# Where a kernel gathers the mean squares of its norms: launch, ends of layers and the second block moved in program order

## The chip, the cores and the metric

The kernel runs on one core of a Trainium2 chip. The metric is device time in microseconds (us) of one execution. Five engines work in order, each through its own row of instructions, and meet at semaphores: PE (TensorE, matmuls), DVE (VectorE), ACT (ScalarE), POOL (GpSimd) and SP (SyncE, which here issues the loads). A row of an engine that waits holds up everything behind it on that engine.

## What is computed

Two transformer blocks over 512 tokens of width 1024, in fp32. The first has two layers of feed-forward, mixed attention, feed-forward; the second has gated mixing, attention and a mixture of experts. Each part begins with a norm over a token's 1024 values:

```python
def rmsnorm(x, g):
    y = xf * lax.rsqrt(jnp.mean(xf * xf, axis=-1, keepdims=True) + EPS)
    return (y * g.astype(jnp.float32)).astype(x.dtype)

def swiglu(h, w_gate, w_up, w_down):
    return (jax.nn.silu(h @ w_gate) * (h @ w_up)) @ w_down

for l in range(DEPTH):          # first block, DEPTH = 2
    x = x + 0.5 * swiglu(rmsnorm(x, ffn1_norm[l]), ...)
    h = rmsnorm(x, mix_norm[l]); ...; x = x + o @ w_out[l]
    x = x + 0.5 * swiglu(rmsnorm(x, ffn2_norm[l]), ...)
return rmsnorm(x, final_norm)   # and the second block begins with rms_norm(h, attn_norm_g)
```

## The kernel before

The activations lie transposed: eight tiles `xT[k]` of 128 features by 512 tokens. The gain is multiplied into the tile before a product, and the factor per token (`rstd`, one over the root of the mean square) is multiplied into the product's result, so that matmuls may start before the norm is known.

An fp32 product is made of three matmuls. `split` turns an operand of 128x1024 into a rounded high part (ACT, `rounded<-base` or `rounded<-ws`, line 407) and the low part, the difference (DVE, line 408); the matmuls are high by high, high by low, low by high. "The cast" and "the low part" below are these two. Three pairs of buffers (`halves`) go round, so a cast waits until matmuls have read the pair three splits back.

**Feed-forward.** `ffn_duo` works on two blocks of columns of the gate and up weights, called a duo here, with seven products (24 matmuls 128x256 each) in place of eight: weights a11, a12, a21, a22 and their sums s1 = a21+a22, s2 = s1-a11, s3 = a11-a21, s4 = a12-s2 (DVE, line 604, `ws`). `cross_tile(q)` makes, for each pair of activation tiles, the operands B11, B2, T12, T34: scaled copies `yc` (ACT, 568), high parts (ACT, 579, 582, 587) and differences (DVE, 560). `down` then multiplies by the down weights (`pd`, lines 414 to 416, 128x512), makes the new tile (DVE, 707, 708), and calls `after(d)`: `norm_tile`, `cross_tile` or, at the end of the fourth feed-forward, `norm_tile2`.

**Norm.** `add_square` squares a tile on ACT (481) and adds it to a running sum on DVE (`acc`, 491). `mean_sq` sums over features with fp32 matmuls by a column of ones (`pstat`, 517), one for each 128 tokens. In the first feed-forward the eight squares are kept apart and all summed by PE: 32 matmuls, each of which shows as two records. `rsqrt` is eleven small operations on DVE (498 to 506). `spread` lays the factor over the partitions: `diag` on DVE (528), a matmul `pspread` on PE (533), a copy `rstd` on ACT (535).

**Launch.** `first_block` loads, in this order on SP's queue, two activation tiles and then half a weight block, four times over, then constants, then the second duo's weights. All eight cross tiles are issued first; then `ffn_duo` splits a11, a12 and s3 and starts three products (`begun`: p1, p2, p3, four steps k each). After three of the four steps comes the whole norm. Then follow s2, s1, s4 (product p4) and a22 (added to p3), and the second duo.

**Second block.** Its norm needs two sums of squares: that of x, and that of x times the final gain (`acc2`, squares at 1371). `second_block` projects k and v, then `gate_products` multiplies by four quarters of weights (`pgv`, 420 to 422: 24 matmuls 128x512 for each quarter), then come both `mean_sq`, two `rsqrt`, `spread`, and the next projections (`pin`, 414 to 416), whose results are multiplied by `rstd` (`ev`, DVE, 753).

Of the kernel before, what the change touches and what calls it, by code (L numbers as in the profile page):

```python
# [86 lines left out]
def layout_first(t):  # L87
    f = np.float32
    out = {}
    out["xt"] = np.ascontiguousarray(t["x"][0].T.reshape(8, 128, S))  # L90
# [221 lines left out]
class Build:  # L312
# [105 lines left out]
    def mm3m(self, out, xh, xl, wh, wl, first, last):  # L418
        mm = self.nc.tensor.matmul
        mm(out, xh, wh, start=first, stop=False)  # L420
        mm(out, xh, wl, start=False, stop=False)  # L421
        mm(out, xl, wh, start=False, stop=last)  # L422
# [54 lines left out]

    def add_square(self, k):

        sq = self.epage("sq") if self.acc_parts is None else self.buffer("sq0", 512, F32, "sq0", 8)  # L480
        self.nc.scalar.activation(sq, self.xT[k], AF.Square)
        if self.acc_parts is None:
            self.acc = self.add_sq(self.acc, sq)
        else:
            self.acc_parts.append(sq)
# [24 lines left out]
    def mean_sq(self, acc, n, eps=True):  # L510
# [3 lines left out]
        parts = acc if isinstance(acc, list) else [acc]  # L514
        for t in range(4):
            for i, a in enumerate(parts):
                nc.tensor.matmul(p[:, t:t + 1], a[:, 128 * t:128 * t + 128], self.ones[:, 0:1], start=i == 0,
                                 stop=i == len(parts) - 1)
# [18 lines left out]

    def rstd_of(self, acc, n):
        col = self.rsqrt(self.mean_sq(acc, n), 4)
# [6 lines left out]
    def start_norm(self):  # L546
        self.XH, self.XL, self.acc, self.acc_parts = [None] * 8, [None] * 8, None, None
# [9 lines left out]
    def cross_tile(self, q, g0):  # L557
# [11 lines left out]
        self.add_square(q)  # L569
# [24 lines left out]
    def ffn_duo(self, wa, wb, acc=None):  # L594
# [3 lines left out]
        a21, a11, a12, a22 = self.first_parts or [self.half_stage(w) for w in (wb[:, :1024], wa[:, :1024], wa[:, 1024:], wb[:, 1024:])]  # L598
        self.first_parts = None
        L, R = slice(0, 256), slice(256, 512)  # L600

        def add(x, y, op):
            z = self.buffer("ws", 1024, F32, "ws", N_WS)
            nc.vector.tensor_tensor(z, x, y, op=op)  # L604
            return z
# [22 lines left out]
        if acc is not None:  # L628
            s3 = add(a11, a21, ALU.subtract)
            begun = [(p1, parts(a11), self.B11, slice(0, 256)), (p2, parts(a12), self.B2, L),  # L630
                     (p3, parts(s3), self.T34, L)]
# [3 lines left out]
            with self.tc.issue_after(mm.ins):  # L635
                _, self.x_rstd = self.rstd_of(acc, D)
# [9 lines left out]
        if acc is None:  # L646
# [1543 lines left out]
```

## Time and profile before

| | |
|---|---|
| Time, median of 3 runs | 2774.12 us (2772.43 to 2777.51) |
| The profiled execution, its own time | 2776.47 us |
| Its span | 2774.6 us |
| Mean granted TensorE clock | 0.979 |
| PE, DVE, ACT busy | 95%, 76%, 51% of the span |

The span runs from the first to the last instruction that the profiler saw; the time holds a little more on both sides. A granted clock of 1.00 is 2.4 GHz, 0.50 is 1.2 GHz.

### The profile page before, as it was taken

Reading aid. Unit: us, or ns where it says so; the run is one execution under the profiler, and the core shown is the slowest. Engines: PE = TensorE matmul, PEld = TensorE weight load, DVE = VectorE, ACT = ScalarE, POOL = GpSimd, SP = SyncE. Lnnn points to the kernel's source line nnn. Section 1 sums busy time; section 2 is a strip of 40 time slices with the busy share of each in tenths; the row PEclk is TensorE's granted clock in tenths of the full one; section 3 lists DMA queues with packets and bytes.
Section 4 is the critical chain, followed back from the end, with each engine's and each line's share of the span. In section 5 each row is a group of like instructions: output and inputs, shape, how many; then the busy total and the mean of one; then the engine's idle time right before and its main releaser. Section 6 shows DMA issues by size and latency. Waiting matters only on the chain. (4 is left out here: it accounts for less than half of the span.)

```text
span 2774.6 us, 39572 instructions
## 1 busy us (share of the span) xinstructions
PE 2637.2 (95%) x15742; PEld 2267.3 (82%) x15742; DVE 2117.2 (76%) x2991; ACT 1401.6 (51%) x2137; POOL 261.8 (9%) x181
## 2 busy tenths in 40 slices
PE   6999999998999998999999999999998999789996
PEld 6999987766899897999987766999996888567774
DVE  6777775687877779787766787878785865579997
ACT  5434346455544355444446465534353644367874
POOL 0000001201000000000002110000000101134442
PEclk9999999999999999999999999999998999889998
DMA  3333331110342322333231111233232223679993
GB/s 126 123 102 88 120 114 63 61 54 22 101 159 92 107 92 84 113 101 107 73 116 55 56 54 33 92 111 94 97 99 96 88 77 120 229 281 365 375 369 124
DMA packets 83698, 335.35 MB, mean 121 GB/s; under 512 B 10414, under 2 KB 11878, under 8 KB 74552
## 3 DMA queue, kind: packets, MB, share of 16 engines
q1 hardware_dynamic: 77096, 315.15, 33.0%
q0 software_dynamic: 5264, 14.51, 1.5%
q8 instruction: 124, 2.03, 0.3%
q10 hardware_dynamic: 1152, 3.15, 0.3%
q14 instruction: 62, 0.51, 0.1%
HBM read 321.93 MB, written 17.84 MB: 122 GB/s over the span
## 5 line engine op out<-in xcount | busy, mean ns | idle before, releaser
L407 ACT CAST rounded<-base 128x1024 fp32r<-128x1024 f32 (+1 forms) x326 | 337.6, 1037 | 468.2 <-PE m L621 164.3
L621 PE MATMUL m<-xt,rounded 128*128 128x256 f32 x4224 | 537.8, 285 | 10.3 <-ACT u L651 5.1
L408 DVE TENSOR_TENSOR rounded<-base,rounded 128x1024 fp32r<-128x1024 f32 (+1 forms) x326 | 401.5, 1232 | 186.6 <-ACT rounded L407 185.5
L621 PEld LDWEIGHTS m<-xt,rounded 128*128 128x128 f32 x4224 | 519.7, 193 | 18.8 <-ACT u L651 6.6
L621 PE MATMUL m<-b,rounded 128*128 128x256 f32 x3168 | 412.6, 286 | 27.6 <-ACT rounded L407 21.8
L621 PEld LDWEIGHTS m<-b,rounded 128*128 128x128 f32 x3168 | 398.6, 194 | 33.7 <-ACT rounded L407 22.1
L408 DVE TENSOR_TENSOR rounded<-ws,rounded 128x1024 fp32r<-128x1024 f32 x176 | 215.3, 1223 | 99.7 <-ACT rounded L407 99.6
L407 ACT CAST rounded<-ws 128x1024 fp32r<-128x1024 f32 x176 | 184.9, 1050 | 197.1 <-PE m L621 108.3
L416 PE MATMUL pd<-h,rounded 128*128 128x512 f32 x704 | 274.8, 391 | 3.4 <-DVE rounded L408 3.4
L415 PE MATMUL pd<-h,rounded 128*128 128x512 f32 x704 | 275.4, 391 | 1.9 <-DVE h L796 1.7
L414 PE MATMUL pd<-h,rounded 128*128 128x512 f32 x704 | 274.6, 390 | 0.0
L414 PE MATMUL pin<-x,rounded 128*128 128x512 f32 x448 | 180.9, 404 | 0.7 <-ACT rstd L535 0.7
L416 PE MATMUL pin<-x,rounded 128*128 128x512 f32 x448 | 178.0, 397 | 0.0
L415 PE MATMUL pin<-x,rounded 128*128 128x512 f32 x448 | 177.4, 396 | 0.4 <-DVE x L476 0.4
L1958 DVE TENSOR_TENSOR rounded<-ew,rounded 128x1024 fp32r<-128x1024 f32 x105 | 167.5, 1614 | 8.2 <-ACT rounded L1956 6.5
L415 PEld LDWEIGHTS pd<-h,rounded 128*128 128x128 f32 x704 | 132.7, 188 | 30.2 <-DVE h L796 3.6
L416 PEld LDWEIGHTS pd<-h,rounded 128*128 128x128 f32 x704 | 132.7, 189 | 30.1 <-DVE rounded L408 3.8
L414 PEld LDWEIGHTS pd<-h,rounded 128*128 128x128 f32 x704 | 132.6, 188 | 26.6
L1956 ACT CAST rounded<-ew 128x1024 fp32r<-128x1024 f32 x119 | 124.9, 1053 | 39.7 <-PE peg L422 16.5
L604 DVE TENSOR_TENSOR ws<-base 128x1024 f32<-128x1024 f32 x88 | 105.8, 1220 | 15.0 <-DMA base<-w_gu 14.9
L1098 POOL TENSOR_TENSOR kpe<-kg,rope 32x512 f32<-32x512 f32 x2 | 2.9, 1459 | 1139.3 <-DVE kg L753 1139.3
L414 PEld LDWEIGHTS pin<-x,rounded 128*128 128x128 f32 x448 | 84.9, 190 | 20.9 <-issue 2.4
(492 smaller groups left out, 4867.4 us busy)
## 6 DMA issues: line engine op xcount, KB each, us to landing
base<-w_gu SPq DMA_DIRECT2D x176, 512.0 KB, 3.9
ew<-e_w SPq DMA_DIRECT2D x154, 512.0 KB, 7.4
base<-w_in SPq DMA_DIRECT2D x27, 1024.0 KB, 4.8
base<-w_dn SPq DMA_DIRECT2D x44, 512.0 KB, 3.7
base<-e_w SPq DMA_DIRECT2D x38, 512.0 KB, 8.5
base<-w_dn SPq DMA_DIRECT2D x16, 1024.0 KB, 4.8
base<-w_o SPq DMA_DIRECT2D x12, 1024.0 KB, 4.8
base<-w_dn SPq DMA_DIRECT2D x8, 768.0 KB, 4.1
```

The costliest lines, as they stand in the source:

```text
L407: nc.scalar.copy(hi[:, :cols], src)
L408: nc.vector.tensor_tensor(lo[:, :cols], src, hi[:, :cols], op=ALU.subtract)
L414: mm(out, wh, xh, start=first, stop=False)
L415: mm(out, wh, xl, start=False, stop=False)
L416: return mm(out, wl, xh, start=False, stop=last)
L604: nc.vector.tensor_tensor(z, x, y, op=op)
L621: mm = nc.tensor.matmul(o, w[:, q], x, start=first and j + k + m == 0, stop=k == 3 and m == 2, skip_group_check=True)
L1098: nc.gpsimd.tensor_tensor(out[r], t[r], self.cm[r], op=ALU.mult)
L1956: nc.scalar.copy(hi, src)
L1958: cut = eng.tensor_tensor(lo, src, hi, op=ALU.subtract)
```

## The change

In five parts. (1) At launch the squares of x come from token rows: a new input `xr` (x itself, four tiles of 128 tokens by 1024) is loaded behind the constants, and four ACT instructions square a row and sum it (`accum_out`). The eight squares of the tiles and the 32 `pstat` matmuls of the launch go. (2) The first three splits (a11, a12, s3) are issued between the cross tiles; the norm's chain and `pspread` stand after product p4. (3) The table of the function silu is loaded ahead of everything (`preload_act_table_set`). (4) At the end of a feed-forward all squares are made, and their sums issued after the last `down` (`add_squares`); after a mixer the sums are issued tile by tile, as before. (5) In the second block the sums of `acc2` are issued after the k and v projections, the `pstat` matmuls and the chain after the first half of `gate_products`, `pspread` after the second half.

```diff
+    def add_squares(self):
+        for sq in self.squares:
             self.acc = self.add_sq(self.acc, sq)
+        self.squares = []
...
+    def mean_sq_rows(self):
+        nc = self.nc
+        v, s = self.small([128, 4], "ms"), self.small([128, 4], "rs_a")
+        for t in range(4):
+            x = self.buffer("xr", 1024, F32, "xr", 2)
+            self.load(x, self.A["xr"][t])
+            with self.tc.issue_after(self.last_hi.ins):
+                nc.scalar.activation(x, x, AF.Square, accum_out=s[:, t:t + 1])
+        nc.vector.tensor_scalar(v, s, 1.0 / D, EPS, op0=ALU.mult, op1=ALU.add)
+        return v
...
-            with self.tc.issue_after(mm.ins):
-                _, self.x_rstd = self.rstd_of(acc, D)
+            if not self.begun:
+                with self.tc.issue_after(mm.ins):
+                    _, self.x_rstd = self.rstd_of(self.acc, D)
...
-        product(p4, parts(s4, u2_copy), self.B2, R)
+        mm = product(p4, parts(s4, u2_copy), self.B2, R)
+        if self.begun:
+            with self.tc.issue_after(mm.ins):
+                _, self.x_rstd = self.rstd_of(self.acc, D)
...
             while pieces:
                 down()
+            if last:
+                self.add_squares()
...
         self.load_constants()
+        self.nc.scalar.preload_act_table_set("silu_and_others")
...
         for q in range(8):
-            self.cross_tile(q, G_FFN1)
+            self.cross_tile(q, G_FFN1, False)
+            if q in (1, 3):
+                begun.append(self.split((a11, a12)[q // 2], 1024))
+            elif q == 5:
+                begun.append(self.split(self.weight_sum(a11, a21, ALU.subtract), 1024))
...
-        self.gate_products()
-        ms1 = self.mean_sq(self.acc, D)
-        ms2 = self.mean_sq(self.acc2, D, eps=False)
+        self.acc2 = None
+        for sq in self.squares2:
+            self.acc2 = self.add_sq(self.acc2, sq)
+        products = self.gate_products()
+        with self.tc.issue_after(next(products).ins):
+            ms1 = self.mean_sq(self.acc, D)
+            ms2 = self.mean_sq(self.acc2, D, eps=False)
...
-        self.rstd = self.spread(self.rcol)
+        with self.tc.issue_after(next(products).ins):
+            self.rstd = self.spread(self.rcol)
```

A scheduler turns the program into the rows of the engines. On ACT at launch, twelve rows in a piece, up to the cast of s2, read before (`yc` is a scaled tile, `sq` a square, `xt` a high part of the last tiles, `rounded<-base` twice are a11 and a12, `rounded<-ws` s3 and then s2):

```order
L568 ACTIVATE yc<-xT_69,base 128x512
L481 ACTIVATE sq_150<-xT_69 128x512
L568 ACTIVATE yc<-xT_69,base 128x512
L587 CAST xt<-yt 128x1024
L481 ACTIVATE sq_153<-xT_69 128x512
L579 CAST b_134<-yc 128x256
L407 CAST rounded<-base 128x1024
L582 CAST b_156<-yc 128x512
L407 CAST rounded<-base 128x1024
L407 CAST rounded<-ws 128x1024
L587 CAST xt<-yt 128x1024
L407 CAST rounded<-ws 128x1024
```

and now (the first row is s3, the pair of `rounded<-ws` s2 and s1, the last row a22; a11 and a12 stand further up, after the first and the second pair of tiles; `xr,base<-xr` are the squares of token rows):

```order
L408 CAST rounded<-ws 128x1024
L588 ACTIVATE yc<-xT_70,base 128x512
L600 CAST b_127<-yc 128x256
L608 CAST xt<-yt 128x1024
L603 CAST b_149<-yc 128x512
L668 COPY m_242<-m_162 128x512
L551 ACTIVATE xr,base<-xr 128x1024 x2
L408 CAST rounded<-ws 128x1024 x2
L608 CAST xt<-yt 128x1024
L551 ACTIVATE xr,base<-xr 128x1024 x2
L408 CAST rounded<-base 128x1024
```

The three first casts have moved up among the tiles; four squares of rows stand where nothing stood, behind the copy m1 of the first product. On SP the four loads of `xr` stand between the second load of constants and the second duo's weights, and wait for no engine.

On DVE at the end of the fourth feed-forward (128x768 is the low part of the third and of the fourth block of down weights, `dx` and `xT` make a new tile, `x` is its low part) there stood before:

```order
L476 SCALAR_TENSOR_TENSOR x_18628<-xT_18624,base,x_18628 128x512
L491 TENSOR_TENSOR acc<-acc,sq 128x512
L708 TENSOR_TENSOR xT_18624<-dx,xT_17731 128x512
L491 TENSOR_TENSOR acc<-acc,sq 128x512
L408 TENSOR_TENSOR rounded<-base,rounded 128x768
L476 SCALAR_TENSOR_TENSOR x_18662<-xT_18624,base,x_18662 128x512
L491 TENSOR_TENSOR acc<-acc,sq 128x512
L408 TENSOR_TENSOR rounded<-base,rounded 128x768
L491 TENSOR_TENSOR acc<-acc,sq 128x512
L408 TENSOR_TENSOR rounded<-base,rounded 128x1024
```

and now:

```order
L708 TENSOR_TENSOR xT_18526<-dx,xT_17610 128x512
L733 SCALAR_TENSOR_TENSOR dx<-pd_18203,rstd 128x512
L409 TENSOR_TENSOR rounded<-base,rounded 128x768
L477 SCALAR_TENSOR_TENSOR x_18530<-xT_18526,base,x_18530 128x512
L734 TENSOR_TENSOR xT_18526<-dx,xT_17610 128x512
L733 SCALAR_TENSOR_TENSOR dx<-pd_18554,rstd 128x512
L409 TENSOR_TENSOR rounded<-base,rounded 128x768
L477 SCALAR_TENSOR_TENSOR x_18546<-xT_18526,base,x_18546 128x512
L734 TENSOR_TENSOR xT_18576<-dx,xT_17695 128x512
L499 TENSOR_TENSOR acc<-sq 128x512
L499 TENSOR_TENSOR acc<-acc,sq 128x512
```

Both low parts now stand ahead of the first sum of squares; before, eight sums stood ahead of the third. The other three ends of feed-forwards move in the same way; the second sum, of `acc2`, now stands after the last tile's low part.

On PE at the second block's norm there stood before:

```order
L420 MATMUL pgv_18803<-rounded,x_18734 128x512
L421 MATMUL pgv_18803<-rounded,x_18734 128x512
L422 MATMUL pgv_18803<-rounded,x_18734 128x512
L517 MATMUL pstat<-base,acc 128x1 x8
L533 MATMUL pspread<-diag,base 128x512
L414 MATMUL pin<-x_18533,rounded 128x512
L415 MATMUL pin<-x_18533,rounded 128x512
L416 MATMUL pin<-x_18533,rounded 128x512
L1585 MATMUL pv_18978<-base,ev 128x128 x4
L414 MATMUL pin<-x_18549,rounded 128x512
```

and now, first at the middle of the gate products and then at their end:

```order
L423 MATMUL pgv_18767<-rounded,x_18546 128x512
L523 MATMUL pstat<-base,acc 128x1 x4
L421 MATMUL pgv_18764<-rounded,x_18580 128x512
L422 MATMUL pgv_18764<-rounded,x_18580 128x512
L523 MATMUL pstat<-base,acc 128x1 x4
L423 MATMUL pgv_18764<-rounded,x_18580 128x512
```

```order
L423 MATMUL pgv_18767<-rounded,x_18674 128x512
L538 MATMUL pspread<-diag,base 128x512
L415 MATMUL pin<-x_18497,rounded 128x512
L416 MATMUL pin<-x_18497,rounded 128x512
L417 MATMUL pin<-x_18497,rounded 128x512
L1623 MATMUL pv_18942<-base,ev 128x128 x4
```

The eight `pstat` matmuls have moved up by two quarters of the products; `pspread` stands behind the last of them. On DVE the small operations moved up with them: one low part stands within them, as before, and two stand between `diag` and the two `ev`.

## Rows read from the trace of the kernel before

**Rows 1.** the page: busy time, share of the span and instructions of each engine

```profile
PE 2637.2 (95%) x15742; PEld 2267.3 (82%) x15742; DVE 2117.2 (76%) x2991; ACT 1401.6 (51%) x2137; POOL 261.8 (9%) x181
```

**Rows 2.** windows, launch: busy us (count) by engine, granted clock, DMA share, GB/s

```profile
10.00:15.00 5.00, 0.00 (x0) 0.00 (x0) 4.56 (x9) 5.00 (x10) 0.00 (x0) 1.00 1.05 415
...
20.00:25.00 5.00, 2.49 (x7) 1.60 (x7) 5.00 (x9) 3.51 (x5) 0.00 (x0) 1.00 0.00 0
...
35.00:40.00 5.00, 5.00 (x27) 5.00 (x26) 0.00 (x0) 0.00 (x0) 0.00 (x0) 0.52 0.00 1
```

**Rows 3.** timeline of PE, launch: start us, us, operation, count, [idle before <-releaser]

```profile
21.14 0.80 PE L621 MATMUL m<-b,rounded 128*128 128x256 f32 x2 [21.14 <-ACT rounded L407]
...
24.90 4.43 PE L621 MATMUL m<-b,rounded 128*128 128x256 f32 x22 [0.55 <-DVE rounded L408]
...
32.29 10.97 PE L517 MATMUL pstat<-base,sq 128*128 128x1 f32 x64
...
52.42 3.13 PE L621 MATMUL m<-xt,rounded 128*128 128x256 f32 x24 [0.64 <-ACT u L651]
...
61.15 1.12 PE L621 MATMUL m<-b,rounded 128*128 128x256 f32 x8
```

**Rows 4.** timeline of DVE, launch

```profile
28.50 1.22 DVE L604 TENSOR_TENSOR ws<-base,ws 128x1024 f32<-128x1024 f32 x1
...
43.29 0.16 DVE L520 TENSOR_SCALAR base<-pstat 128x4 f32<-128x4 f32 x1 [13.57 <-PE pstat L517]
...
48.72 0.69 DVE L528 TENSOR_TENSOR diag<-base 128x512 f32<-128x512 f32 x1
...
53.83 1.23 DVE L408 TENSOR_TENSOR rounded<-ws,rounded 128x1024 fp32r<-128x1024 f32 x1 [0.69 <-ACT rounded L407]
```

**Rows 5.** timeline of ACT, launch

```profile
3.96 1.28 ACT L568 ACT_TABLE_LOAD   x1 [3.96 <-DMA xT<-xt]
...
5.88 0.61 ACT L481 ACTIVATE sq<-xT 128x512 f32<-128x512 f32 x1
```

**Rows 6.** groups of ACT by line and form: count, busy us, mean ns

```profile
L930 ACT ACTIVATION_READ_ACCUMULATOR p<-s,base 128x1 f32 x144 | 28.5, 198 | 0.0
```

**Rows 7.** timeline of PE, DVE and ACT before the second block

```profile
2076.90 0.82 ACT L407 CAST rounded<-base 128x768 fp32r<-128x768 f32 x1
...
2088.14 0.69 DVE L491 TENSOR_TENSOR acc<-acc,sq 128x512 f32<-128x512 f32 x1
...
2088.74 0.95 DVE L408 TENSOR_TENSOR rounded<-base,rounded 128x768 fp32r<-128x768 f32 x1
...
2089.75 0.55 PE L416 MATMUL pd<-h,rounded 128*128 128x512 f32 x1 [3.35 <-DVE rounded L408]
...
2090.10 0.63 PE L414 MATMUL pd<-h,rounded 128*128 128x512 f32 x1
```

**Rows 8.** timeline of PE, DVE and ACT at the second block's norm

```profile
2131.61 0.95 PE L517 MATMUL pstat<-base,acc 128*128 128x1 f32 x8
...
2140.81 2.04 PE L533 MATMUL pspread<-diag,base 128*128 128x512 f32 x2 [6.95 <-DVE diag L528]
...
2145.68 0.77 PE L414 MATMUL pin<-x,rounded 128*128 128x512 f32 x1
...
2122.01 1.23 DVE L408 TENSOR_TENSOR rounded<-base,rounded 128x1024 fp32r<-128x1024 f32 x1 [4.21 <-ACT rounded L407]
...
2127.45 1.23 DVE L408 TENSOR_TENSOR rounded<-base,rounded 128x1024 fp32r<-128x1024 f32 x1 [4.21 <-ACT rounded L407]
...
2143.51 1.29 DVE L753 TENSOR_TENSOR ev<-pin,rstd 128x512 f32<-128x512 f32 x2 [2.84 <-ACT rstd L535]
...
2131.81 1.04 ACT L407 CAST rounded<-base 128x1024 fp32r<-128x1024 f32 x1 [4.38 <-PE pgv L422]
...
2142.89 0.59 ACT L535 COPY rstd<-pspread 128x512 f32<-128x512 f32 x1 [10.04 <-PE pspread L533]
```

**Rows 9.** timeline of PE between the second and third feed-forward

```profile
1067.95 7.38 PE L621 MATMUL m<-b,rounded 128*128 128x256 f32 x44 [2.58 <-DVE rounded L408]
```

More of the change, by code (lines that the diff above doesn't have):

```diff
@@ L89, in layout_first @@
     out = {}
+    out["xr"] = np.ascontiguousarray(t["x"][0].reshape(4, 128, D))
     out["xt"] = np.ascontiguousarray(t["x"][0].T.reshape(8, 128, S))
@@ L421, in mm3m @@
         mm(out, xh, wl, start=False, stop=False)
-        mm(out, xl, wh, start=False, stop=last)
+        return mm(out, xl, wh, start=False, stop=last)
     def const(self, name, dt=F32):
@@ L513, in mean_sq @@
         p = self.bank("pstat")
-        parts = acc if isinstance(acc, list) else [acc]
         for t in range(4):
-            for i, a in enumerate(parts):
-                nc.tensor.matmul(p[:, t:t + 1], a[:, 128 * t:128 * t + 128], self.ones[:, 0:1], start=i == 0,
-                                 stop=i == len(parts) - 1)
+            nc.tensor.matmul(p[:, t:t + 1], acc[:, 128 * t:128 * t + 128], self.ones[:, 0:1], start=True, stop=True)
         v = self.small([128, 4], "ms")
@@ L536, in spread @@
         return r
+    def mean_sq_rows(self):
[8 more added lines that the diff above has]
+        return v
     def rstd_of(self, acc, n):
+        if acc is None:
+            col = self.rsqrt(self.mean_sq_rows(), 4)
+            return col, self.spread(col)
         col = self.rsqrt(self.mean_sq(acc, n), 4)
@@ L555, in clear, with cross_tile @@
         self.load(self.YD[128 * j:128 * j + 128], self.A["k_zero"])
-    def cross_tile(self, q, g0):
+    def cross_tile(self, q, g0, squares=True):
         nc = self.nc
@@ L568, in cross_tile @@
         nc.scalar.activation(y[:, o:o + 512], self.xT[q], AF.Copy, scale=self.gcol(g0 + q))
-        self.add_square(q)
+        if squares:
+            self.add_square(q)
         if q % 2 == 0:
@@ L592, in cross_tile, with weight_sum, ffn_duo @@
         self.T34.append((th[:, 512:], tl[:, 512:]))
-    def ffn_duo(self, wa, wb, acc=None):
+    def weight_sum(self, x, y, op):
+        z = self.buffer("ws", 1024, F32, "ws", N_WS)
+        self.nc.vector.tensor_tensor(z, x, y, op=op)
+        return z
+    def ffn_duo(self, wa, wb, first=False):
         nc = self.nc
-        a21, a11, a12, a22 = self.first_parts or [self.half_stage(w) for w in (wb[:, :1024], wa[:, :1024], wa[:, 1024:], wb[:, 1024:])]
-        self.first_parts = None
+        a21, a11, a12, a22 = self.loaded or [self.half_stage(w) for w in (wb[:, :1024], wa[:, :1024], wa[:, 1024:], wb[:, 1024:])]
+        self.loaded = None
         L, R = slice(0, 256), slice(256, 512)
[L602 to L605, printed above, removed]
+        add = self.weight_sum
         def parts(a, after=None):
@@ L627, in ffn_duo @@
         c, d = self.buffer("c", 1024, F32, "d", N_D), self.buffer("d", 1024, F32, "d", N_D)
[L628 to L631, printed above, removed]
+        if first:
+            w11, w12, w3 = self.begun or (parts(a11), parts(a12), parts(add(a11, a21, ALU.subtract)))
+            begun = [(p1, w11, self.B11, slice(0, 256)), (p2, w12, self.B2, L), (p3, w3, self.T34, L)]
             for k in range(3):
@@ L645, in ffn_duo @@
         m1_copy = nc.scalar.copy(m1, p1)
-        if acc is None:
+        if not first:
             product(p3, parts(s3), self.T34, L)
@@ L651, in ffn_duo @@
         u2_copy = nc.scalar.copy(u2, p1)
-        if acc is None:
+        if not first:
             product(p2, parts(a12, m1_copy), self.B2, L)
@@ L1364, in norm_tile2 @@
         if k == 0:
-            self.acc2 = None
+            self.squares2 = []
             self.gg = self.fixed("gg", [128, 8])
@@ L1369, in norm_tile2 @@
         self.add_square(k)
-        sq2 = self.epage("sq")
-        nc.scalar.activation(sq2, self.xT[k], AF.Square, scale=self.gcol(G_FIN + k))
-        self.acc2 = self.add_sq(self.acc2, sq2)
+        self.squares2.append(self.square(k, self.gcol(G_FIN + k)))
     def proj2(self, name):
```

26 lines of the change are left out of this document (14 added, 12 removed).

## The prediction

> **What bounds the kernel now.** I read the page first: PE is busy 95% of the span [rows 1], so time can only come from PE's waits and from work on PE that is not needed or runs at a low clock. Then I went along PE's timeline and noted each wait; those near the change lie in four places.
>
> At the launch PE's first matmul waits until 21.14 for a cast; at 32.29 it begins 64 records of sums of squares that take 10.97 us, and the second duo starts at 61.15 [rows 3]. From 35 to 40 the granted clock is 0.52 and neither DVE nor ACT does anything [rows 2]; DVE's idle stretch of 13.57 us ends with those sums [rows 4]. So the stretch is one chain: sums on PE, small operations on DVE, then the low parts of s2, s1, a22 and s4, that of s4 last (53.83 [rows 4]), then product p4.
>
> Before the second block PE waits 3.35 us at 2089.75 for the low part of the third block of down weights. Its cast was done at 2077.72 (2076.90 + 0.82), but the low part ran at 2088.74, right behind a sum of squares [rows 7]: it was queued, not late. Then matmuls take 0.63 each at half clock.
>
> At the second block's norm the gate products end at 2131.61; PE sums squares, waits 6.95 us for the chain on DVE that ends in `diag`, spreads, and has its projections going again at 2145.68 [rows 8], 14.07 us later. During the products DVE idles 4.21 us ahead of each low part [rows 8].
>
> Between the second and third feed-forward PE waits too (2.58 us [rows 9]), in a stretch where DVE works without a break, with the same sums in its row.
>
> **The launch.** Removed: 32 matmuls on PE (10.97 us) [rows 3] and eight squares on ACT (0.61 each) [rows 5]. Added: four loads of 512 KB, and on ACT four squares of 128x1024 with a sum. No such square is in the trace. It is bounded below by a cast of that size (1.04) [rows 8] and above by that and a separate read of the sum (0.20) [rows 6], a little over 1.2; I take 1.25 and so 2.5 for the two that stand ahead of s2's cast. The table load (1.28 on ACT ahead of the first tile) [rows 5] goes to the time before any data is there.
>
> What ends last now is DVE's row, which I followed in its new order. Before, everything ahead of s2's low part was done at 29.72 (28.50 + 1.22) [rows 4], with DVE busy 5.00 of 5 us from 20 to 25 [rows 2]. Now the same rows stand ahead, without the low part of the last pair of tiles (1.23), with the addition c (0.69), and all may begin 1.28 earlier: 29.72 - 1.23 + 0.69 - 1.28 = 27.9. On ACT I added up the rows in order: m1's copy ends at some 24.5, two row squares at 27.0, the cast near 28.5. I take 28.7 for the start of s2's low part. Behind it stand, in order: low part of s2, of s1, of the tiles, and s4 (4 x 1.23 = 4.9, to 33.6); twelve small operations (2.3, to 35.9, from the 6.95 us [rows 8], in which DVE did 26 of them, a low part and `diag`: (6.95 - 1.23 - 0.69)/26 = 0.19 each); `diag` (0.69, to 36.6); low parts of a22 and s4 (2.46, to 39.1). Before, s4's ended at 55.06: 16 us gained. Behind it all is as before but for `pspread`, now between p4 and a22's product: 2.04 at half clock [rows 8], half of that at full. **Minus 15 us**; from 18 (the ACT copies and squares hide, the pipelined pitch of DVE is 0.1 shorter per row) down to 7, the case of the low clock below.
>
> The first operation of the new chain waits on DVE for the fourth row square; queued behind it are the low parts of a22 and s4, hence PE. That square is ready if its row is there by about 30. The four rows follow the constants in SP's queue: 2.1 MB at 415 GB/s is 5 us, and the queue was idle from 20 to 25 [rows 2]. The second duo's weights come 5 us later than before, still well ahead of a duo that starts near 45.
>
> *Clock.* Matmuls from 24.90, the first dense ones, take 4.43 us for 22, 0.20 each, against 3.13 for 24, 0.13 each, from 52.42 [rows 3], though the granted clock reads 1.00 in both. So the start of dense work is slow whatever the column says. In the new order PE has some 70 matmuls spread thin from 11 to 28, and the dense stretch begins at 28.7. Some 3 us at 0.20 cost 1 to 1.5 us, which DVE's chain up to 39.1 hides.
>
> The Trainium skill's page "TensorE: Matmul & The Clock Gate" (Part 1) says that the throttled clock is the default and that only sustained activity lifts it; by that rule thinly spread matmuls could keep the clock low through the whole first duo, which is rival A. The trace agrees as far as the 0.20 goes.
>
> The skill's page "ScalarE: Activation LUTs" (What ACT_TABLE_LOAD costs) gives some 2.7 us for a table load; by that the launch term would be 16.4 instead of 15. The row here shows 1.28, and the sum goes by it.
>
> **Ends of feed-forwards.** The sums are as many as before, 0.69 each on DVE, but stand behind the low parts. Before the second block eight of them no longer precede the third low part, 8 x 0.69 = 5.5 us, more than the 3.35 us of wait. What is late next is the fourth low part, whose cast waits for PE; DVE has only tile work ahead of it. So the wait goes whole, and with it the half clock: eight matmuls at a pitch of 0.43 (2090.10 on) [rows 7] instead of 0.23 (the products' 5.44/24) [rows 8] are 1.6 us. **Minus 5 us**; bounds 0 (a tile's low part ends last anyway) and 6.
>
> Between second and third feed-forward the stretch is bound by all that DVE does, and nothing of that is removed; sums and low parts change places, and a wait of 1.2 (one low part) may come at the last tiles. I take minus 0.5, bounds -3 and +2. After the first and third feed-forward PE had no wait to lose; the covering work there is PE's own products. After the mixers the sums stay tile by tile: 0.
>
> **The second block's norm.** The chain from the end of the first sum to `diag` now starts after the second quarter of products. Two quarters are left, 10.88 us (2 x 5.44, the pitch of the low parts) [rows 8]; the chain took from 2131.61 to 2140.81, 9.2 us, so it fits, with 1.7 to spare, in DVE's idle time. The 16 records of sums (2.0 us) stay on PE's path, amid the products. What is left behind the products, from their end T: `pspread` (1.0 at full clock); ACT casts from T + 0.2 to T + 1.24 as now [rows 8], then copies `rstd` (0.59, to T + 1.9); DVE takes the low part of that cast (1.23, to T + 2.5), then the two `ev` (1.29, to T + 3.8); transposes (0.6); projections at T + 4.4. Before it was T + 14.07 with the sums in it: 14.07 - 4.4 - 2.0 = 7.7, and 1.2 more for five matmuls at half clock behind 2145.68, of which I keep 0.8, since waits of 2 us remain. **Minus 8.5 us**; bounds 5 (`pspread` at half clock, and the clock falls as before) and 10.
>
> **Sum.** 15 + 5 + 0.5 + 8.5 = 29 from the profiled execution's 2776.47: 2747.5. That execution lay 2.35 above the median of its three runs, so the number to hold against 2774.12 is **2745 us**, 1.05% faster. A change within 0.2%, 5.5 us, counts as no difference here.
>
> **Rivals.**
> A. *The clock stays low through the first duo.* For: 0.20 per matmul from 24.90 on, and the clock of 0.52 in a stretch in which PE was 5.00 of 5 us busy [rows 2]. Against: before, dense matmuls reached 0.13 within the same first duo. All products of duo 1 from 28.7 on at double time put the second duo at 54 in place of 45.7: the launch gains 7, sum 21, 2753 us. Chance 0.12.
> B. *Another wait takes the place of the low part before the second block*, or the later sums stall the boundary of the second and third feed-forward by 2: 5 to 7 less, 2750 to 2752. For: DVE is the busiest helper there. Against: the wait was queueing alone. 0.12.
> C. *The second norm is only half hidden*, because the chain meets a low part that waits for a cast (a low part stands amid the small operations) or starts late behind the `acc2` sums: 4 less, 2749. 0.1.
> D. *Slower.* The rows come late: DVE waits at the chain's first operation and holds a22 and s4 behind it. It needs 2.1 MB to take until 60 us, which is 49 GB/s in place of 415 [rows 2], before the whole gain of 29 is gone; past that the kernel is slower than before, at 62 already by 2 us (2776). 0.02.
> E. *Most of it is given back*: rivals A to C together, which leaves 29 - 8 - 7 - 4 = 10 and with a stall in the second duo less than 5: 2764 to 2772. 0.04.
>
> **How the numbers follow.** My forecast has 0.6, between 2738 (18 + 6 + 3 + 10 = 37) and 2749. The range 2737 to 2755 adds A, B and C and leaves out 0.1 to 0.2 at the ends. Faster by over 0.2%: 0.95 (forecast, A, B, C, and a part of E); within: 0.03 (E); slower: 0.02 (D).
>
> **What would show it.** In the trace after: PE's first matmul near 11; p4 near 39.3 and the second duo's first product near 45.7; no granted clock of 0.5 between 35 and 49; the low part of s4 last before p4, with no wait of DVE for a row square. No wait of over 1 us on PE at the third block of down weights. `pspread` directly behind the last gate product, and under 5 us from there to the steady projections. It would be wrong if the first duo's matmuls stay at 0.20 past 35, if the row squares end after 34, or if the rows that the change leaves alone move by several us.

## The result and the profile after

The changed kernel takes 2743.98 us (median of 4 runs, 2742.02 to 2747.63) where the kernel before takes 2774.14 (4 runs): 0.989 of its time, interval 0.987 to 0.991. The forecast was 2745. The profiled execution took 2744.27, its span is 2742.2, so the spans differ by 32.4 us.

To see where the 32.4 us went I compare the start of the same instruction in both traces: silu on ACT (44 pairs in the first block) and the first gate activation of the second block. From one such instruction to the next, the difference moves by:

| stretch of the program | forecast | after |
|---|---|---|
| launch and first two duos (to 360 us before) | -15 | -14.3 |
| first mixer and the duo after it (to 738.7) | 0 | -3.5 |
| second feed-forward but its end (to 1032.9) | 0 | +0.4 |
| end of the second feed-forward (1032.9 to 1096.0) | -0.5 | -0.8 |
| third feed-forward (to 1391.8) | 0 | -1.1 |
| second mixer, fourth feed-forward (to 2063.9) | 0 | -0.3 |
| end of the fourth feed-forward, to the second block | -5 | -5.2 |
| second block's norm (to 2146.7) | -8.5 | -7.8 |
| rest | 0 | +0.3 |

The split between the last two places is at the cast behind the second quarter of gate products (2120.93 before, 2096.06 after). The page, busy time by engine, in place of [rows 1]:

```profile
PE 2619.7 (96%) x15678; PEld 2249.7 (82%) x15678; DVE 2118.0 (77%) x2991; ACT 1399.9 (51%) x2136; POOL 262.1 (10%) x181
```

PE does 17.5 us less, DVE and ACT almost the same (0.8 more, 1.7 less).

**Launch.** Windows, in place of [rows 2]:

```profile
30.00:35.00 5.00, 4.33 (x24) 4.33 (x25) 4.63 (x14) 1.57 (x4) 0.00 (x0) 0.66 0.20 59
...
35.00:40.00 5.00, 3.50 (x29) 3.29 (x28) 4.12 (x5) 2.48 (x3) 0.00 (x0) 1.00 0.76 232
```

The window from 35 to 40, in which DVE and ACT did nothing, is now full of work; the low clock has shrunk to a part of the window from 30 to 35. PE's timeline, in place of [rows 3]:

```profile
10.12 0.79 PE L644 MATMUL m<-b,rounded 128*128 128x256 f32 x2 [10.12 <-ACT rounded L408]
...
30.67 4.86 PE L644 MATMUL m<-xt,rounded 128*128 128x256 f32 x27 [0.76 <-DVE rounded L409]
...
37.04 3.13 PE L644 MATMUL m<-xt,rounded 128*128 128x256 f32 x24 [1.50 <-ACT u L674]
...
40.01 3.04 PE L644 MATMUL m<-b,rounded 128*128 128x256 f32 x24
...
46.62 3.04 PE L644 MATMUL m<-b,rounded 128*128 128x256 f32 x24
```

The first matmul runs at 10.12, the second duo at 46.62 in place of 61.15: 14.5 us. Product p4 starts at 40.01. The chain of DVE and ACT that leads there, in place of [rows 4, 5]:

```profile
28.26 2.36 DVE L409 TENSOR_TENSOR rounded<-ws,rounded 128x1024 fp32r<-128x1024 f32 x2
...
32.80 0.17 DVE L552 TENSOR_SCALAR base<-base 128x4 f32<-128x4 f32 x1
...
35.20 0.69 DVE L533 TENSOR_TENSOR diag<-base 128x512 f32<-128x512 f32 x1
...
36.53 1.23 DVE L409 TENSOR_TENSOR rounded<-base,rounded 128x1024 fp32r<-128x1024 f32 x1 [0.64 <-ACT rounded L408]
...
37.97 1.23 DVE L409 TENSOR_TENSOR rounded<-ws,rounded 128x1024 fp32r<-128x1024 f32 x1 [0.21 <-ACT rounded L408]
...
9.03 1.04 ACT L408 CAST rounded<-base 128x1024 fp32r<-128x1024 f32 x1 [2.02 <-DMA base<-w_gu]
...
24.46 1.06 ACT L551 ACTIVATE xr<-xr 128x1024 f32<-128x1024 f32 x1
...
25.42 0.19 ACT L551 ACTIVATION_READ_ACCUMULATOR xr<-xr 128x1 f32 x1
...
35.46 1.04 ACT L408 CAST rounded<-base 128x1024 fp32r<-128x1024 f32 x1 [3.89 <-PE m L644]
...
36.41 0.58 ACT L674 COPY u<-m 128x512 f32<-128x512 f32 x1
```

DVE runs from s2's low part to the end of `diag` without a wait, and the first small operation (32.80) has waited for nothing: the last row square was done at 31.6. A row square takes 1.06 and its reading 0.19. ACT waited 2.02 us for the first weights at 9.03. The low part of s4 ends at 39.20; but p4 starts at 40.01, right behind the product before it, which had started at 37.04 after PE had waited 1.50 us for the copy u2, itself behind 27 matmuls that took 4.86 us at 0.18 each. DVE's last two low parts hang on the same 27 matmuls: the cast of a22 (35.46) waited 3.89 us for PE, until they ended, and the low parts of a22 (36.53) and s4 (37.97) waited 0.64 and 0.21 us for their casts.

**Before the second block**, in place of [rows 7], DVE and ACT:

```profile
2058.77 0.95 DVE L409 TENSOR_TENSOR rounded<-base,rounded 128x768 fp32r<-128x768 f32 x1
...
2061.74 0.96 DVE L409 TENSOR_TENSOR rounded<-base,rounded 128x768 fp32r<-128x768 f32 x1
...
2063.88 0.68 DVE L499 TENSOR_TENSOR acc<-sq 128x512 f32<-128x512 f32 x1
...
2057.90 0.82 ACT L408 CAST rounded<-base 128x768 fp32r<-128x768 f32 x1
```

The third low part (2058.77) starts 0.05 us after its cast ended; the first sum of squares (2063.88) stands behind the fourth. PE has no wait left there.

**Second block's norm**, in place of [rows 8]:

```profile
2095.86 0.94 PE L523 MATMUL pstat<-base,acc 128*128 128x1 f32 x8
...
2108.61 1.02 PE L538 MATMUL pspread<-diag,base 128*128 128x512 f32 x2
...
2112.36 1.01 PE L1623 MATMUL pv<-base,ev 128*128 128x128 f32 x4 [1.01 <-DVE ev L781]
...
2113.02 0.78 PE L415 MATMUL pin<-x,rounded 128*128 128x512 f32 x1
...
2104.08 0.69 DVE L533 TENSOR_TENSOR diag<-base 128x512 f32<-128x512 f32 x1
...
2109.88 1.23 DVE L409 TENSOR_TENSOR rounded<-base,rounded 128x1024 fp32r<-128x1024 f32 x1 [3.97 <-ACT rounded L408]
...
2111.02 1.28 DVE L781 TENSOR_TENSOR ev<-pin,rstd 128x512 f32<-128x512 f32 x2
...
2108.80 1.04 ACT L408 CAST rounded<-base 128x1024 fp32r<-128x1024 f32 x1 [4.38 <-PE pgv L423]
...
2109.76 0.58 ACT L540 COPY rstd<-pspread 128x512 f32<-128x512 f32 x1
```

`diag` is done at 2104.77, 3.8 us before it is needed. Behind the last product (T = 2108.61) come `pspread`, the copy behind the cast (2109.76, T + 1.2), the low part, `ev` (T + 2.4), the transposes (T + 3.8) and the projections at T + 4.41; 4.4 was forecast.

**Between second and third feed-forward**, in place of [rows 9]:

```profile
1052.63 5.82 PE L644 MATMUL m<-b,rounded 128*128 128x256 f32 x26 [5.38 <-DVE rounded L409]
```

The waits of PE have run together: 5.38 in one place, where 2.58, 0.86, 1.43 and 0.84 stood.

### The profile page after: what moved, and what is told of

Same layout as the page of the kernel before. It is cut to its first block, busy times and chain, and to the rows that moved or that the text cites. A ratio compares the mean times of both kernels' runs of the same rounds, so it can differ in the third digit from the quotient of the medians.

```text
span 2742.2 us, 39469 instructions
## 1 busy us (share of the span) xinstructions
PE 2619.7 (96%) x15678; PEld 2249.7 (82%) x15678; DVE 2118.0 (77%) x2991; ACT 1399.9 (51%) x2136; POOL 262.1 (10%) x181
## 5 line engine op out<-in xcount | busy, mean ns | idle before, releaser
L1994 ACT CAST rounded<-ew 128x1024 fp32r<-128x1024 f32 x119 | 124.8, 1052 | 40.1 <-PE peg L423 16.6
L617 DVE TENSOR_TENSOR ws<-base 128x1024 f32<-128x1024 f32 x88 | 105.7, 1220 | 14.5 <-DMA base<-w_gu 14.5
L415 PEld LDWEIGHTS pin<-x,rounded 128*128 128x128 f32 x448 | 84.9, 189 | 20.1 <-issue 2.7
```

The source lines that it names most:

```text
L415: mm(out, wh, xh, start=first, stop=False)
L617: self.nc.vector.tensor_tensor(z, x, y, op=op)
L1994: nc.scalar.copy(hi, src)
```

## The experiments

Twelve runs, one of them the changed kernel again. Four kernels ran once (chain late, rows loaded late, extra matmuls, no early table load), so their times are single values. Starts are compared as above, with those of the kernel before; times with the kernel before on the same chip (2776.0, 2775.8 and 2776.5 us in the three groups).

| kernel | fourth silu pair, 106 us | second pair behind the first mixer, 761 | 2041 | second block, 2147 | time, us |
|---|---|---|---|---|---|
| after | -14.4 | -17.8 | -19.6 | -32.7 | 2743.98 |
| after, again | -15.5 | -18.9 | -20.1 | -33.4 | 2745.61 |
| launch alone | -15.0 | -17.5 | -19.1 | -24.0 | 2755.80 |
| late sums alone | -0.6 | -4.4 | -4.3 | -9.5 | 2770.23 |
| norm amid products alone | -1.1 | -1.1 | +0.7 | -7.5 | 2770.01 |
| own buffers for squares alone | -0.1 | 0.0 | -2.3 | -7.3 | 2772.88 |
| early splits alone | -3.8 | -3.7 | -3.2 | -3.2 | 2772.38 |
| after, tile squares | +2.4 | -1.2 | -2.8 | -15.8 | 2759.97 |
| after, chain late | -10.3 | -12.7 | -12.9 | -26.0 | 2750.67 |
| after, rows loaded late | -8.1 | -10.6 | -12.0 | -25.0 | 2751.62 |
| after, extra matmuls | -15.5 | -19.1 | -20.8 | -33.9 | 2742.89 |
| after, no early table load | -14.5 | -16.6 | -20.3 | -33.7 | 2742.19 |
| after, one cast held | -14.1 | -16.0 | -17.5 | -31.6 | 2745.31 |

**Launch alone.** Sums and second norm put back:

```diff
-        self.squares.append(self.square(k))
+        self.acc = self.add_sq(self.acc, self.square(k))
...
-        with self.tc.issue_after(next(products).ins):
-            ms1 = self.mean_sq(self.acc, D)
+        list(products)
+        ms1 = self.mean_sq(self.acc, D)
```

> The launch's parts alone (row squares, early splits, table load ahead, chain after p4); sums of squares and the second block's norm stay as in the kernel before. By my reasons each part is worth its own: the second duo starts near 46.6 as in the changed kernel, some 14.4 us earlier than before, nothing else moves, time 2759 to 2760. Rival one: the launch's gain is given back later (a stall in the second duo or at the first down weights): under 10 us, 2764 or more. Rival two, on the 3.5 us that the changed kernel gained between the first and the third feed-forward, outside my sum: if they hang on the new order of sums, they are missing here; if they are luck of the clock, they may come or not.

The time is 0.9929 of the kernel before (0.9912 to 0.9945), 20 us, more than the 15 expected. The launch gives 15.0; 2.8 came in the first mixer, and 4.9 at the end of the fourth feed-forward, where the wait of 3.35 us has gone although the sums are issued at once again. What this kernel keeps of the change there is that squares have sixteen buffers of their own.

**Late sums alone.** In the kernel before, `add_square` collects, and `add_squares` sums after the last `down`; `acc2` after the k and v projections; sixteen buffers `sq` as in the change.

```diff
         if self.acc_parts is None:
-            self.acc = self.add_sq(self.acc, sq)
+            self.squares.append(sq)
...
             while pieces:
                 down()
+            if last:
+                self.add_squares()
```

> The late sums of squares alone (ends of feed-forwards; the second sum after the k and v projections), launch and second norm's place as before. By my reasons PE's wait of 3.35 us for the third block of down weights before the second block goes with its low clock, 5 us, and the boundary of the second and third feed-forward gives 0.5 to 1: time 2768. Rival: another wait takes its place, as a low part of the last tile behind the sums: 0 to 2 us gained, 2772 to 2774. If the 3.5 us gained in the first mixer come from this part, 2765.

0.9978 (0.9969 to 0.9988). The end of the fourth feed-forward gives 5.2, as expected; another 3.8, in the first mixer, again lie where nothing was forecast.

**Norm amid the products alone.**

```diff
-        self.gate_products()
-        ms1 = self.mean_sq(self.acc, D)
-        ms2 = self.mean_sq(self.acc2, D, eps=False)
+        products = self.gate_products()
+        with self.tc.issue_after(next(products).ins):
+            ms1 = self.mean_sq(self.acc, D)
+            ms2 = self.mean_sq(self.acc2, D, eps=False)
...
-        self.rstd = self.spread(self.rcol)
+        with self.tc.issue_after(next(products).ins):
+            self.rstd = self.spread(self.rcol)
```

> The second block's norm amid its gate products alone; all sums where they were. By my reasons the wait of 6.95 us on PE goes, the projections run some 7.5 us earlier: time 2766 to 2767. Rival: the gain needs the late sums too, since the chain starts behind them: 3 us or less, 2771 or more.

0.9974 (0.9964 to 0.9983). From 2041 to 2147 this kernel gains 8.1 us: the part needs no other. The medians differ by 6.0 and the spans of the profiled executions by 5.4, since 0.7 was lost before that place and 2.1 behind it, where the program is as before.

**The changed kernel again.**

> The changed kernel unchanged, once more, to see what differs from one execution's trace to the next. If the 3.5 us gained in the first mixer and the 1 us in the third feed-forward are the program's, the same stretches show them again, at the same places, with time 2744. If they are luck of the clock, the low-clock stretches in the mixers (three there before, one in the first mixer after) fall elsewhere and the third duo set starts 14 to 18 us earlier than before instead of 17.8; the launch and the second norm stay as they are.

The first mixer shows its 3.4 us again and the third feed-forward its 0.9; the second mixer has three low stretches of the clock in this execution and two in the other. At the second block's norm the clock stays at 1.00 in this execution, and the stretch from 2041 to 2147 gains 13.4 where the other gained 13.0.

**Own buffers.** The kernel before with this alone:

```diff
-        sq = self.epage("sq") if self.acc_parts is None else self.buffer("sq0", 512, F32, "sq0", 8)
+        sq = self.buffer("sq", 512, F32, "sq", 16) if self.acc_parts is None else self.buffer("sq0", 512, F32, "sq0", 8)
...
-        sq2 = self.epage("sq")
+        sq2 = self.buffer("sq", 512, F32, "sq", 16)
```

> The kernel before, with one thing changed: squares of the layer ends have sixteen buffers of their own in place of the six that they share with the running sum and diag. Sums are still issued right behind each square. If the six shared buffers are what put the sums ahead of the third low part, the wait of 3.35 us before the second block goes and 5 us with it: 2771 where the kernel before takes 2776. If the place at which the sums are issued does it, as my prediction says, nothing changes: 2776.

0.9989 (0.9980 to 0.9999). The medians differ by 2.9 us only, between the 5 and the nothing of the two expectations, and its ten executions spread from 2768.86 to 2776.34; so the place is read from the trace. From 2041 to 2147 it gains 5.0 us. DVE before the second block:

```profile
2074.89 1.29 DVE L491 TENSOR_TENSOR acc<-sq 128x512 f32<-128x512 f32 x2
...
2077.30 0.95 DVE L408 TENSOR_TENSOR rounded<-base,rounded 128x768 fp32r<-128x768 f32 x1
...
2078.83 1.28 DVE L491 TENSOR_TENSOR acc<-acc,sq 128x512 f32<-128x512 f32 x2
...
2081.24 0.95 DVE L408 TENSOR_TENSOR rounded<-base,rounded 128x768 fp32r<-128x768 f32 x1
```

The sums still run as the squares come, two at a time, but the low parts of the third and fourth block (2077.30, 2081.24) now stand among them and not behind them.

**Early splits alone.** The kernel before, with `begun` filled between the cross tiles as in the change.

> The kernel before with the three first splits issued between the tiles, all else (tile squares, 32 matmuls with ones after three of four steps, table load) as before. By my reasons the started products end some 6 us earlier and the sums on PE begin near 26 instead of 32.3; the second duo starts at 52 to 55 instead of 61.2, 6 to 9 us gained. Rival: DVE's row is as long as before and the splits only move: under 2 us gained.

0.9983 (0.9974 to 0.9993); 3.8 us at the fourth silu pair, neither the 6 to 9 nor the under 2; the second duo starts at 57.10. PE:

```profile
26.06 11.28 PE L517 MATMUL pstat<-base,sq 128*128 128x1 f32 x64
...
38.41 7.61 PE L621 MATMUL m<-xt,rounded 128*128 128x256 f32 x30
```

The sums begin at 26.06 as expected, 6.2 us earlier, and take 11.28 us. But the clock falls during them and stays low over the products that follow (38.41: 30 in 7.61, 0.25 each); its windows:

```profile
31.00:36.00 5.00, 5.00 (x25) 5.00 (x25) 0.00 (x0) 0.00 (x0) 0.00 (x0) 0.50 0.00 0
...
36.00:41.00 5.00, 4.78 (x20) 4.19 (x20) 2.90 (x7) 1.99 (x2) 0.00 (x0) 0.50 0.00 0
```

**Tile squares in the new order.** The changed kernel with eight squares of tiles and 32 matmuls with ones, behind p4:

```diff
-            self.cross_tile(q, G_FFN1, False)
+            self.cross_tile(q, G_FFN1)
...
         self.begun = begun
+        self.acc = self.squares
```

> The changed kernel with the eight squares of tiles and their 32 matmuls with ones back, in the place of the row squares (behind product p4). By my reasons these matmuls stand on PE's path: 8 to 11 us, with ACT's squares 1 or 2 more; the second duo starts at 55 to 58 in place of 46.6, time 2754 to 2757. Rival: the early splits are the gain and the matmuls hide in waits of PE: second duo before 50, time under 2749.

0.9937 (0.9920 to 0.9954). The second duo starts at 57.94, as expected:

```profile
41.56 11.69 PE L525 MATMUL pstat<-base,sq 128*128 128x1 f32 x64
...
53.12 4.98 PE L647 MATMUL m<-xt,rounded 128*128 128x256 f32 x24
...
57.94 3.04 PE L647 MATMUL m<-b,rounded 128*128 128x256 f32 x24
```

But the whole loss against the changed kernel is 16.8 us at the fourth silu pair: the sums take 11.69 us on PE, a22's product runs behind the sums at a granted clock of 0.50 (53.12: 24 in 4.98), and the second duo then waits another 2.74 us for a late `rstd`. So the row squares are worth more than the matmuls they replace.

**Chain late.**

```diff
-            with self.tc.issue_after(mm.ins):
+            with self.tc.issue_after(mm.ins), self.tc.issue_after(self.last_lo.ins):
                 _, self.x_rstd = self.rstd_of(self.acc, D)
```

where `last_lo` is the low part of s4.

> The changed kernel with the twelve small operations, diag and pspread placed behind the low parts of a22 and s4 on DVE. In my prediction DVE's row ahead of the low part of s4 sets product p4, and these operations are 3 us of it: p4 then starts 2 to 3 us earlier than at 40.0 and the second duo near 44. Rival, from the trace after: p4 waits for PE's own product before it, which ran slowly behind a wait: p4 stays at 40.0, the second duo near 46, and the factor rstd, now late, may cost something in the second duo.

```profile
39.42 3.04 PE L644 MATMUL m<-b,rounded 128*128 128x256 f32 x24
...
54.62 4.39 PE L644 MATMUL m<-xt,rounded 128*128 128x256 f32 x24 [2.67 <-ACT m L668]
...
35.95 1.23 DVE L409 TENSOR_TENSOR rounded<-base,rounded 128x1024 fp32r<-128x1024 f32 x1 [3.92 <-ACT rounded L408]
...
52.14 0.69 DVE L693 TENSOR_TENSOR c<-c,rstd 128x512 f32<-128x512 f32 x1 [1.91 <-ACT rstd L540]
```

The first matmul of this run was at 9.28, and p4 came 30.1 us behind it; after, 29.9 (40.01 - 10.12). The small operations out of DVE's way do not bring p4 forward: the rival holds. DVE, free of them, waits 3.92 us (35.95) for the cast of a22, which waits for PE, and the low part of s4 ends 29.3 us behind the first matmul (after, 29.1). And `rstd` now ends so late that DVE waits 1.91 us for it at 52.14; the copy m that PE needs stands on ACT behind the silu of these results, and PE waits 2.67 us. The kernel loses 5.0 us against the changed kernel run again: -10.3 against -15.5, less the 0.2 by which its first matmul came later (9.28, there 9.06).

**Rows loaded late.** The second duo's weights are loaded ahead of the token rows:

```diff
         if self.begun:
+            wa, wb = self.A["w_gu"][0, 2], self.A["w_gu"][0, 3]
+            self.loaded = [self.half_stage(w) for w in (wb[:, :1024], wa[:, :1024], wa[:, 1024:], wb[:, 1024:])]
```

> The changed kernel with the four loads of token rows behind all four loads of the second duo's weights on SP's queue, two of which wait for buffers. By my reasons the rows have some 5 to 8 us to spare; the two weights that wait for buffers hold them longer than that, so the first small operation waits on DVE, product p4 or a22 comes later and the second duo starts 3 to 10 us later than at 46.6, time 2748 to 2755. Rival: the weights' buffers come free early enough and nothing moves: 2744 to 2746.

```profile
40.22 3.04 PE L644 MATMUL m<-b,rounded 128*128 128x256 f32 x24
...
45.98 3.04 PE L644 MATMUL m<-b,rounded 128*128 128x256 f32 x24
...
56.52 5.40 PE L644 MATMUL m<-xt,rounded 128*128 128x256 f32 x24 [3.19 <-ACT m L668]
...
39.06 1.06 ACT L551 ACTIVATE xr<-xr 128x1024 f32<-128x1024 f32 x1 [0.93 <-DMA xr<-xr]
```

The rows come at 39, the scheduler puts the chain behind the low parts, and p4 (40.22) and the second duo (45.98) are not late at all. The price comes in the second duo, where PE waits 3.19 us and then runs at half pace (56.52: 24 in 5.40): 6.3 us. Size as expected, place not. It shows too that the row squares ahead of s2's cast do not hold up p4: without them it came 30.4 us behind the first matmul (9.82), within the 29.8 to 30.8 of the kernels whose launch is that of the changed kernel (29.8 in the repeat, 30.7 in the launch alone, 30.8 with one cast held).

**Extra matmuls.** Twenty matmuls 128x256 into p4's bank, overwritten later, where PE waits for s2's cast:

```diff
+        if self.begun:
+            (wh, wl), (bh, bl) = w12, self.B2[3]
+            for i in range(20):
+                fill = nc.tensor.matmul(p4[:, :256], wh[:, 384:512], bh[:, :256], start=True, stop=True, skip_group_check=True)
```

> The changed kernel with twenty extra matmuls (128x256, their result is overwritten) where PE waits 2.4 us for s2's cast at the launch, so that it does not go idle. If the low clock from 30 to 34 comes from that wait and holds up product p4, the stretch stays at 1.00, p4 starts 1 to 2 us earlier than the 29.9 us after the first matmul, and so does the second duo. Rival: the clock falls anyway, or DVE's row (the low part of s4) keeps p4 where it is: under 0.5 us.

```profile
29.46 4.86 PE L644 MATMUL m<-xt,rounded 128*128 128x256 f32 x27 [0.88 <-DVE xt L580]
...
38.85 3.04 PE L644 MATMUL m<-b,rounded 128*128 128x256 f32 x24
```

```profile
27.00:32.00 5.00, 3.42 (x14) 3.02 (x15) 4.93 (x7) 4.19 (x7) 0.00 (x0) 0.71 0.75 214
```

A miss: the wait of 2.4 us is filled and the clock falls all the same (0.71 from 27 to 32); 27 matmuls take 4.86 as in the changed kernel, and p4 comes 30.0 us behind the first matmul (8.83). Shorter waits stay on PE, the last of 0.88 us ahead of the 27 matmuls.

**No early table load.** `preload_act_table_set` left out.

> The changed kernel without the table load ahead of everything: ACT loads a table in front of the first tile and silu's in the first duo. My prediction counts 1.28 us for it at the head of the chain: p4 and the second duo then come 1 to 1.3 us later. Rival, from the trace after, in which ACT and DVE wait 2 us for the first weights behind the first pair of tiles: the load hides there and nothing at the launch moves (under 0.3 us).

The fourth silu pair is 14.5 us earlier than before, against 14.4 with the load ahead. In this execution the first weights came earlier, the first cast ran at 7.39 without a wait, and p4 came 31.1 us behind the first matmul, 1.2 more than with the load ahead. That 1.2 is not the table's: the granted clock is 0.50 from 29 to 35 in this execution, where it was low from 30 to 34 in the other, and the 27 matmuls take 6.13 us in place of 4.86. The load hides wherever ACT waits for the first weights anyway, as it did after (2.02 us). With one profiled execution of each, and weights that come at different times, what the part is worth is not settled; at the fourth silu pair the two are within 0.1 us.

**One cast held.** In the second block, the third cast behind `spread` is issued after the copy `rstd`.

```diff
+        self.hold = getattr(self, "hold", 0) - 1
+        with ExitStack() as es:
+            if self.hold == 0:
+                es.enter_context(self.tc.issue_after(self.rstd_copy.ins))
+            nc.scalar.copy(hi[:, :cols], src)
```

> The changed kernel with one cast of the second block's projections placed behind the copy rstd on ACT, and with it its low part behind the two ev on DVE. In my prediction that cast and that low part are 1.0 and 1.2 us of the 4.4 us that are left behind the gate products: the projections then resume 1 to 2 us earlier, and the time is 2743 to 2745, within what the measurement can tell from the changed kernel. Rival: the copy waits for pspread as long as for the cast, and the next projections need the held low part: no change, or 1 us worse.

From 2041 to 2147 it gains 14.1 against 13.0 of the changed kernel: the 1.1 is there in the trace. Some 0.4 of it is the clock, which does not fall in that stretch here, as in the repeat (13.4); 0.7 is left for the cast, a little under the 1 to 2 expected. The time, 2745.31, does not tell the two apart; no version here is shown to beat the changed kernel.

## Why the prediction held, point by point

**Launch: 15 forecast, 14.5 at the second duo.** Removing the sums from PE and having the splits early both count, and not as a sum: early splits alone give 3.8, the row squares taken away from the changed kernel cost 16.8. The sums cost more than their own time: in all three kernels the products behind them run slowly (12 in 2.91 us from 43.12 in the kernel before, 30 in 7.61 with early splits, 24 in 4.98 with tile squares; 24 take 3.13 in the changed kernel). That the two parts need each other is not shown in full, since no run has the row squares without the early splits.

The low part of s4 was forecast to end at 39.1 and ended at 39.2, which is luck: `diag` was done 0.7 us ahead of the forecast (35.89 for 36.6), and 0.85 us of waits for casts, which the sum has not, came behind it. The step that failed is "What ends last now is DVE's row", and with it "Some 3 us at 0.20 cost 1 to 1.5 us, which DVE's chain up to 39.1 hides." It does not hide them: PE's own row, the slow product of s2, the copy u2, the next product, ends at 40.01 and sets p4, 0.8 us behind DVE's. DVE's row does not set itself either: the cast of a22 waits 3.89 us until PE's 27 matmuls end, most likely for one of the three pairs of buffers, a wait that the sum left out. That the small operations on DVE stand on the path, as I had it, is refuted by the chain put late, where DVE waits for that cast instead (3.92 us).

Rival A, a clock that stays low through the first duo, did not come: the granted clock is 0.69, 0.50, 0.50 and 0.60 in the four microseconds from 30 to 34 and 1.00 from there, and 24 matmuls take 3.13 from 37.04 on. The Trainium skill's page "TensorE: Matmul & The Clock Gate" (Part 1) says that the throttled clock is the default and only sustained activity lifts it; the trace agrees for the first dense stretch alone (0.18 each from 30.67), and ahead of it, with PE idle or thinly used, the profile shows 1.00.

Rival D, rows that come late, has its price from the late loads: 6.3 us for rows at 39 and not, as I had it, a standstill of DVE. A standstill depends on where the scheduler puts the first small operation.

**Ends of feed-forwards: 5 forecast, 5.2.** The size is right and so is the wait. The step that failed is its cause: the sums "stand behind the low parts" because they are issued later. With own buffers alone and sums issued at once, the wait goes as well (5.0, and 4.9 in the launch alone). No run issues the sums later on the six shared buffers, so whether the place alone would do it is open. In the kernel before, squares, running sum and `diag` shared six buffers; that the scheduler put each sum ahead to free one is my reading of this, and not shown by itself. At the boundary of second and third feed-forward it is 0.8 for 0.5, with waits moved and not removed. Rival B, another wait in place of the low part, did not come: PE has none before the second block.

**Second norm: 8.5 forecast, 7.8 after and 8.1 alone.** The chain was hidden with 3.8 us to spare, against rival C, and the path behind the products was right to 0.1 us. What was mis-sized is the clock: I kept 0.8 us of a saving at the projections, but they run again at half pace (0.78 and 0.63 each from 2113.02). In the repeat they run at 0.48 and 0.39 each from 2112.36, at a granted clock of 1.00, and the place gives 8.1.

**Not forecast: 4.9 us gained elsewhere and 0.7 given back**, 3.5 of the gain in the first mixer. That the median still came out within 1 us of the forecast is partly luck. The profiled executions differ by 32.2 us where the sum has 29; the medians differ by 30.2, because the profiled execution of before lay 2.3 us above its median and that of after 0.3. The last section has what is known of the gains elsewhere.

## What to carry to other kernels

Before crediting an instruction's new place with the removal of a wait, look at what it no longer shares: here six shared buffers went along with the order on DVE, and a change of two lines that gave the squares buffers of their own gave the same 5 us. A sum over partitions by fp32 matmuls with one column is paid for twice, in its own time and in the clock of what follows; sums along the free axis on ScalarE, from a second layout of the input, took both away, for four more loads of 512 KB. And a forecast by one engine's row should be held against the other engines' rows to the same point: here DVE's and PE's ended within 0.8 us of each other, the end of DVE's hung on casts that waited for PE, and taking 3 us of work out of DVE's gave nothing.

## What the runs showed of the hardware

With the very same rows of instructions the second mixer took 3.0 us less in the kernel with own buffers than in the kernel before. The difference lies in the clock. Windows of the kernel before and then of the one with own buffers, which runs 0.3 us later at the first of them:

```profile
1665.00:1675.00 10.00, 9.09 (x46) 7.31 (x46) 9.26 (x14) 3.81 (x8) 3.34 (x3) 0.83 0.00 0
...
1685.00:1695.00 10.00, 8.78 (x43) 6.96 (x43) 7.23 (x13) 4.22 (x9) 1.80 (x2) 0.83 0.01 2
...
1700.00:1710.00 10.00, 7.28 (x40) 4.98 (x39) 4.30 (x12) 2.74 (x7) 0.00 (x0) 0.83 0.00 0
```

```profile
1665.00:1675.00 10.00, 8.82 (x43) 7.01 (x43) 9.31 (x14) 3.67 (x7) 3.35 (x4) 0.83 0.00 0
...
1685.00:1695.00 10.00, 8.71 (x56) 6.67 (x57) 7.64 (x14) 4.35 (x10) 2.05 (x2) 1.00 0.01 2
...
1700.00:1710.00 10.00, 7.00 (x42) 4.73 (x43) 4.86 (x13) 2.72 (x6) 0.00 (x0) 1.00 0.00 0
```

Three low stretches stand against one. In the first mixer the same two kernels have three each and agree to 0.1 us, while the launch alone, with the same rows there, has one and gains 2.8. So waits of the same length on PE lower the clock at one time and not at another, and a mixer here is uncertain by 3 us from that alone. Of the twelve other executions, the seven with one low stretch in the first mixer gain 2.2 to 3.8 us in it; of the five with two, the chain put late and the rows loaded late gain 2.4 and 2.5, one cast held 2.0, early splits nothing, and the norm amid products, in which one of the two lasts twice as long, 0.3. So the count of low stretches goes with the gain and does not give its size. Whether the changed rows at the mixers' ends add some tenths is open.

PE's records say 5.00 of 5 us busy while matmuls of one column run, yet the clock falls 2.1 to 3.4 us behind their start in each of the six kernels that have 64 records of them (32.29 before, 26.06 with early splits, 41.56 with tile squares), and stays low for 10 to 17 us. It falls at the launch of the eight kernels without them too, between 26 and 31, but there for 3 to 7 us; so the fall with early splits may not be the sums' doing, while that at 43.7 with tile squares, right behind two dense products, is hard to lay to anything else. The 16 such records amid the gate products leave it at 1.00.
